# Row normalization on one core: 16 tiles of 8 rows in six buffers, in place of tiles of 12 rows in four

## The chip, the cores and the metric

The kernel runs on one core of a Trainium2 chip. The core has several engines with instruction queues of their own. Three matter here: DVE (VectorE), which does the arithmetic; ACT (ScalarE), which does a little of it and issues the stores; and SP (SyncE), which issues the loads. The transfers themselves run on 16 DMA engines that both queues share. The metric is the time of one execution on the device, in microseconds (us); lower is better.

## The reference

```python
def setup_inputs():
    batch, seq, dim = 32, 512, 1024
    return {"x": np.random.randn(batch, seq, dim).astype(np.float32)}

def reference(x):
    sums = np.sum(np.abs(x), axis=-1, keepdims=True)
    return (x / (sums + 1e-8)).astype(np.float32)
```

Each of the 16384 rows of 1024 floats (4 KB) is divided by the sum of its absolute values. Input and output are 67.11 MB each, and every byte is read once and written once.

## The kernel before

The 16384 rows are spread over the 128 partitions of the on-chip memory, so each partition has 128 rows to do, in 11 tiles: ten of 12 rows per partition (48 KB) and a last one of 8 rows (32 KB). Four tile buffers (`BUFS = 4`) hold 4 x 48 KB = 192 KB of each partition.

The function `piece` says which rows of the input and output a tile covers. The first 128 x 32 rows are the head: in it each partition owns 32 consecutive rows, which make up tiles 0 and 1 (12 rows each) and the last tile (8 rows). Behind the head each tile of 12 rows is a block of its own, in which each partition owns 12 consecutive rows. A row of a partition in the tile thus starts 128 KB from the next partition's in the head, and 48 KB behind it.

`load(i)` (line 82) issues a tile's load on SP, `store(i)` (line 85) its store on ACT. Both limit the contiguous piece that one DMA packet moves to 24576 bytes: a tile of 12 rows goes out as two packets of 24 KB per partition, and the tile of 8 rows as two of 16 KB. One transfer is spread over the 16 DMA engines, 8 partitions on each.

`normalize` computes a tile in place: a reduction over the rows on DVE (line 47), two small instructions on the sums (lines 54 and 56, adding the epsilon and taking the reciprocal), and then the products. The table `split` gives for a tile how its rows are shared out. By default one DVE instruction multiplies all rows by their reciprocals (line 58). For tiles 0, 1, 2 and the last two, some rows are instead done one at a time, by DVE (line 65) or by ACT (line 68); an entry (3, 4) means three rows by line 65 and four by line 68.

The order is written out by hand: four loads first, then for each tile compute, store, and the load of the tile four further on. That load reuses the buffer, so SP waits until the store from that buffer has landed. DVE waits for each tile's load; ACT issues a store when the tile's products are done. The loads form one queue (q1 in the profile), the stores another (q10).

Of the kernel before, what the change touches and what calls it, by code (L numbers as in the profile page):

```python
# [1 line left out]

# [4 lines left out]

FP32 = mybir.dt.float32
EPS = 1e-8


@with_exitstack
def kernel(
    ctx: ExitStack,
    tc: tile.TileContext,
    x: bass.AP,
    out: bass.AP,
):
    nc = tc.nc
    P = nc.NUM_PARTITIONS  # L20

    x_flat = x.flatten_outer_dims()
    out_flat = out.flatten_outer_dims()
    n, d = x_flat.shape

    R = 12
    BUFS = 4
    HEAD = 32
    per_partition = n // P
    assert n % P == 0 and (per_partition - HEAD) % R == 0  # L30
    rows = [R] * ((per_partition - HEAD) // R + 2) + [HEAD - 2 * R]

    def piece(flat, i):
        head = flat[: P * HEAD, :].rearrange("(p r) d -> p r d", p=P)
        if i < 2:
            return head[:, R * i : R * (i + 1), :]
        if i == len(rows) - 1:
            return head[:, 2 * R :, :]
        a = P * (HEAD + R * (i - 2))
        return flat[a : a + P * R, :].rearrange("(p r) d -> p r d", p=P)  # L40

    sbuf = ctx.enter_context(tc.tile_pool(name="sbuf", bufs=BUFS))
    stats = ctx.enter_context(tc.tile_pool(name="stats", bufs=len(rows)))

    def normalize(x_tile, k, kv, kt):
        s = stats.tile([P, R], FP32)
        nc.vector.tensor_reduce(  # L47
            out=s[:, :k],
            in_=x_tile[:, :k, :],
            axis=mybir.AxisListType.X,  # L50
            op=mybir.AluOpType.add,
            apply_absolute_value=True,
        )
        nc.vector.tensor_scalar_add(out=s[:, :k], in0=s[:, :k], scalar1=EPS)  # L54
        inv = stats.tile([P, R], FP32)
        nc.vector.reciprocal(out=inv[:, :k], in_=s[:, :k])  # L56
        if kv:
            nc.vector.tensor_mul(  # L58
                out=x_tile[:, :kv, :],
                in0=x_tile[:, :kv, :],  # L60
                in1=inv[:, :kv].unsqueeze(2).to_broadcast([P, kv, d]),
            )
        for r in range(kv, kv + kt):
            row = x_tile[:, r, :]
            nc.vector.tensor_scalar_mul(out=row, in0=row, scalar1=inv[:, r : r + 1])  # L65
        for r in range(kv + kt, k):
            row = x_tile[:, r, :]
            nc.scalar.activation(  # L68
                out=row,
                in_=row,  # L70
                func=mybir.ActivationFunctionType.Copy,
                scale=inv[:, r : r + 1],
            )

    last = len(rows) - 1
    split = {0: (3, 4), 1: (0, 3), 2: (0, 3), last - 1: (0, 2), last: (5, 3)}

    tiles = {}

    def load(i):  # L80
        x_tile = tiles[i] = sbuf.tile([P, R, d], FP32, name="x_tile")
        nc.sync.dma_start(out=x_tile[:, : rows[i], :], in_=piece(x_flat, i), max_dma_last_dim=24576)  # L82

    def store(i):
        nc.scalar.dma_start(out=piece(out_flat, i), in_=tiles[i][:, : rows[i], :], max_dma_last_dim=24576)

    def compute(i):
        k = rows[i]
        kt, ks = split.get(i, (0, 0))
        normalize(tiles[i], k, k - kt - ks, kt)  # L90

    with tc.manual_schedule():
        for i in range(BUFS):
            load(i)
        for i in range(len(rows)):
            compute(i)
            store(i)
            if i + BUFS < len(rows):
                load(i + BUFS)


# [1 line left out]
_INS = ['x']  # L103
_OUTS = [((32, 512, 1024), 'float32')]


# [23 lines left out]
```

## Time and profile before

| | |
|---|---|
| time, median of 3 runs | 316.91 us (316.88 to 317.0) |
| time of the profiled execution | 316.94 us |
| its span | 315.3 us |
| DVE busy | 261.2 us, 83% of the span |
| ACT busy | 17.4 us, 6% |
| DMA queue of the loads, share of the 16 engines' span | 49.9% |
| DMA queue of the stores | 49.4% |
| bytes moved | 134.22 MB, 426 GB/s over the span |
| load of a tile of 12 rows, issue to landing (median) | 37.3 us |
| store of a tile of 12 rows, issue to landing (median) | 47.4 us |

The span runs from the first to the last instruction that the profile shows; the time of the execution is slightly more. Busy time on an engine is the sum of its instructions. The shares of the two DMA queues count the time of their packets against 16 engines over the whole span, so that together they tell how full the DMA engines were. In tables by window, each line gives a stretch of the span, the busy time of DVE, ACT and POOL in it (with the number of instructions), a clock that plays no part here, the DMA share and the rate at which bytes moved. In tables of instructions, `s` are the sums, `inv` the reciprocals, and the shapes are partitions x elements.

### The profile page before, as it was taken

The numbers are of one execution on the slowest core, as the hardware profiler recorded it, in microseconds if no ns is written. First come the engines' busy times: TensorE is split into PE (matmuls) and PEld (weight loads), VectorE is DVE, ScalarE is ACT, GpSimd is POOL, SyncE is SP. The second block draws the span as 40 slices with busy tenths as digits, with TensorE's granted clock in tenths as the row PEclk, the third lists the DMA queues.
The fourth block names the chain that finished last, engine by engine and source line by source line (L and its number), as shares of the span: only waits on it lengthen the run. The fifth ranks groups of instructions, "written<-read, shape, count | busy, mean of one in ns | idle before, by whom it ended". The sixth has DMA issues, their size and how long they took to land.

```text
span 315.3 us, 168 instructions
## 1 busy us (share of the span) xinstructions
DVE 261.2 (83%) x51; ACT 17.4 (6%) x16; POOL 0.2 (0%) x4
## 2 busy tenths in 40 slices
DVE  0079999999999999979996997999699969999100
ACT  0010503004000000000000000000000000203000
POOL 0000000000000000000000000000000000000000
DMA  7999999999999999999999999999999999999997
GB/s 299 449 440 408 449 393 415 440 449 418 430 449 418 430 449 418 430 449 421 427 449 421 427 449 424 424 449 433 415 449 436 412 448 419 446 417 449 440 408 333
DMA packets 5984, 134.22 MB, mean 426 GB/s; under 512 B 352, under 2 KB 352, under 8 KB 352
## 3 DMA queue, kind: packets, MB, share of 16 engines
q1 hardware_dynamic: 2992, 67.11, 49.9%
q10 hardware_dynamic: 2992, 67.11, 49.4%
HBM read 67.11 MB, written 67.11 MB: 426 GB/s over the span
## 4 chain that ended last, share of the span: by engine, by line
DVE 41%; DMA 33%; another core or an unknown queue 18%; SPq 0%; issue 0%; DVEq 0%
DVE s L47 23%; DMA x_tile<-in_x_dram 17%; DVE x_tile L58 15%; DMA out_dram<-x_tile 15%; DVE x_tile L65 1%; DVE inv L56 0%; DVE s L54 0%; SPq L82 0%; DVEq L125 0%
## 5 line engine op out<-in xcount | busy, mean ns | idle before, releaser
L47 DVE TENSOR_REDUCE s<-x_tile 128x12 f32<-128x12288 f32 (+1 forms) x11 | 138.2, 12562 | 30.1 <-DMA x_tile<-in_x_dram 30.1
L58 DVE TENSOR_TENSOR x_tile<-x_tile,inv 128x12288 f32<-128x12288 f32 (+3 forms) x10 | 113.6, 11358 | 0.5
L68 ACT ACTIVATE x_tile<-x_tile,inv 128x1024 f32<-128x1024 f32 x15 | 16.1, 1138 | 257.1 <-DVE inv L56 257.1
L65 DVE TENSOR_SCALAR x_tile<-x_tile,inv 128x1024 f32<-128x1024 f32 x8 | 5.5, 747 | 0.0
L56 DVE RECIPROCAL inv<-s 128x12 f32<-128x12 f32 (+1 forms) x11 | 2.5, 225 | 0.4
L68 ACT ACT_TABLE_LOAD x1 | 1.3, 1283 | 17.9 <-DMA x_tile<-in_x_dram 17.9
L54 DVE TENSOR_SCALAR s<-s 128x12 f32<-128x12 f32 (+1 forms) x11 | 1.9, 172 | 0.4
L114 POOL MEMSET const-bfloat16-1.0<- 128x1 bf16 x1 | 0.1, 101 | 0.0
L114 POOL MEMSET const-uint8-127<- 128x1 uint8 x1 | 0.1, 101 | 0.0
L114 POOL MEMSET const-float32-0.0<- 128x1 f32 x1 | 0.1, 98 | 0.2 <-issue 0.2
L114 POOL MEMSET const-float32-1.0<- 128x1 f32 x1 | 0.1, 98 | 0.0
## 6 DMA issues: line engine op xcount, KB each, us to landing
x_tile<-in_x_dram SPq DMA_DIRECT2D x10, 6144.0 KB, 37.3
out_dram<-x_tile ACTq DMA_DIRECT2D x10, 6144.0 KB, 47.4
x_tile<-in_x_dram SPq DMA_DIRECT2D x1, 4096.0 KB, 32.5
out_dram<-x_tile ACTq DMA_DIRECT2D x1, 4096.0 KB, 21.6
```

What stands on the lines that cost most here:

```text
L47: nc.vector.tensor_reduce(out=s[:, :k], in_=x_tile[:, :k, :], axis=mybir.AxisListType.X, op=mybir.AluOpType.add, apply_absolute_value=True,)
L54: nc.vector.tensor_scalar_add(out=s[:, :k], in0=s[:, :k], scalar1=EPS)
L56: nc.vector.reciprocal(out=inv[:, :k], in_=s[:, :k])
L58: nc.vector.tensor_mul(out=x_tile[:, :kv, :], in0=x_tile[:, :kv, :], in1=inv[:, :kv].unsqueeze(2).to_broadcast([P, kv, d]),)
L65: nc.vector.tensor_scalar_mul(out=row, in0=row, scalar1=inv[:, r : r + 1])
L68: nc.scalar.activation(out=row, in_=row, func=mybir.ActivationFunctionType.Copy, scale=inv[:, r : r + 1],)
L114: nc = _bacc.Bacc("TRN2", target_bir_lowering=False, num_devices=1)
```

## The change

All tiles now have 8 rows per partition: 16 equal tiles instead of eleven, in six buffers of 32 KB instead of four of 48 KB (again 192 KB per partition). The limit on the packet size is gone from the load and the store, so the 32 KB that a partition contributes to a tile are one contiguous piece for one descriptor. The head is gone too. Instead, every three consecutive tiles form a group in which each partition owns 24 consecutive rows (96 KB); the sixteenth tile is a group by itself, in which a partition owns 8 rows (32 KB). In `split`, the entries for tiles 0, 1 and 2 are smaller, in keeping with the smaller tiles; those of the last two tiles stay. The reduction, the small instructions and the loops are as before.

```diff
-    R = 12
-    BUFS = 4
-    HEAD = 32
+    R = 8
+    BUFS = 6
+
+    GROUP = 3
     per_partition = n // P
-    assert n % P == 0 and (per_partition - HEAD) % R == 0
-    rows = [R] * ((per_partition - HEAD) // R + 2) + [HEAD - 2 * R]
+    assert n % P == 0 and per_partition % R == 0
+    rows = [R] * (per_partition // R)
 
     def piece(flat, i):
-        head = flat[: P * HEAD, :].rearrange("(p r) d -> p r d", p=P)
-        if i < 2:
-            return head[:, R * i : R * (i + 1), :]
-        if i == len(rows) - 1:
-            return head[:, 2 * R :, :]
-        a = P * (HEAD + R * (i - 2))
-        return flat[a : a + P * R, :].rearrange("(p r) d -> p r d", p=P)
+        g = i // GROUP
+        size = min(GROUP, len(rows) - g * GROUP) * R
+        a = P * g * GROUP * R
+        j = (i - g * GROUP) * R
+        own = flat[a : a + P * size, :].rearrange("(p r) d -> p r d", p=P)
+        return own[:, j : j + R, :]
...
-    split = {0: (3, 4), 1: (0, 3), 2: (0, 3), last - 1: (0, 2), last: (5, 3)}
+    split = {0: (2, 3), 1: (0, 2), 2: (0, 2), last - 1: (0, 2), last: (5, 3)}
...
-        nc.sync.dma_start(out=x_tile[:, : rows[i], :], in_=piece(x_flat, i), max_dma_last_dim=24576)
+        nc.sync.dma_start(out=x_tile[:, : rows[i], :], in_=piece(x_flat, i))
...
-        nc.scalar.dma_start(out=piece(out_flat, i), in_=tiles[i][:, : rows[i], :], max_dma_last_dim=24576)
+        nc.scalar.dma_start(out=piece(out_flat, i), in_=tiles[i][:, : rows[i], :])
```

## The prediction, on record before the changed kernel ran

> **What bounds the kernel now.** I read the page first: who is busy, and whether the DMA engines ever stop.
>
> ```profile
> DVE 261.2 (83%) x51; ACT 17.4 (6%) x16; POOL 0.2 (0%) x4
> DMA  7999999999999999999999999999999999999997
> DMA packets 5984, 134.22 MB, mean 426 GB/s; under 512 B 352, under 2 KB 352, under 8 KB 352
> q1 hardware_dynamic: 2992, 67.11, 49.9%
> q10 hardware_dynamic: 2992, 67.11, 49.4%
> ```
>
> The two queues (q1 the loads of SP, q10 the stores of ACT) fill 99.3% of the 16 DMA engines' time, against 83% of DVE's. Of 5984 packets 352 are tiny: one per engine at the end of each of 22 transfers. The other 5632 are 352 for each engine, 320 of 24 KB (twenty transfers of 12 rows: 8 partitions, two each) and 32 of 16 KB (two of 8 rows). So the end is set by how long an engine takes for its packets, and by the time in which it has none. The windows show both; their last two columns are DMA share and GB/s.
>
> ```profile
> 0.00:4.00 4.00, 0.00 (x0) 0.00 (x0) 0.20 (x4) 1.00 0.62 197
> 40.00:44.00 4.00, 4.00 (x1) 0.00 (x0) 0.00 (x0) 1.00 0.95 319
> 60.00:240.00 180.00, 169.54 (x28) 3.23 (x3) 0.00 (x0) 1.00 1.00 433
> 305.20:312.50 7.30, 0.00 (x0) 0.00 (x0) 0.00 (x0) 1.00 1.00 431
> ```
>
> From 60 to 240 us, all 24 KB packets, the rate is flat at 433 GB/s: 16 x 24576 B / 433 = 908.1 ns per packet on an engine. At the end, all 16 KB packets, it is 431: 608.2 ns. An engine's packets therefore take 320 x 908.1 + 32 x 608.2 ns = 310.05 us. The head loses 2.2 us (197 x 4 / 433 = 1.8 us of work in 4), and the stretch at 40 us, where the first store's packets join the loads, 1.05 us. That makes 313.3; the remaining 2.0 us of the 315.3 lie behind the last packets. The program's own time in this execution is 316.94, 1.64 around the span and 0.03 over the median shown.
>
> Then the costs on DVE by shape, and the end in order of time, since only there can the queue run dry.
>
> ```profile
> L47 DVE TENSOR_REDUCE s<-x_tile 128x12 f32<-128x12288 f32 x10 | 129.5, 12949 | 30.1 <-DMA x_tile<-in_x_dram 30.1
> L58 DVE TENSOR_TENSOR x_tile<-x_tile,inv 128x9216 f32<-128x9216 f32 x2 | 19.5, 9758 | 0.1
> L58 DVE TENSOR_TENSOR x_tile<-x_tile,inv 128x5120 f32<-128x5120 f32 x1 | 5.5, 5491 | 0.0
> L65 DVE TENSOR_SCALAR x_tile<-x_tile,inv 128x1024 f32<-128x1024 f32 x8 | 5.5, 747 | 0.0
> L47 DVE TENSOR_REDUCE s<-x_tile 128x8 f32<-128x8192 f32 x1 | 8.7, 8686 | 0.0
> ```
>
> ```profile
> 280.01 8.69 DVE L47 TENSOR_REDUCE s<-x_tile 128x8 f32<-128x8192 f32 x1
> 280.11 0.38 ACTq L85 DMA_DIRECT2D out_dram<-x_tile  x1
> ...
> 289.18 3.40 DVE L65 TENSOR_SCALAR x_tile<-x_tile,inv 128x1024 f32<-128x1024 f32 x5
> 292.66 0.38 ACTq L85 DMA_DIRECT2D out_dram<-x_tile  x1
> ```
>
> DVE waits 30.1 us for loads, none the other way in mid-run. The last store goes out at 292.66, when some 20.6 us of packets are left (to 313.3), of which its own are 32/2 x 0.608 = 9.7: it came 11 us before the queue would have been empty.
>
> **The change, part by part.** *Packets.* An engine has 256 of 32 KB in place of 352. No row has one of 32 KB. From both sides: by the straight line through the two sizes 908.1 + (908.1 - 608.2) = 1208.0 ns; in proportion, with no fixed part saved, 908.1 x 4/3 = 1210.8. The 431 is rounded and its window short, so I take the middle, 1209.4: 256 x 1209.4 = 309.61 us, a gain of 0.45 (0.8 at one end, 0.1 at the other).
>
> The Trainium skill ("DMA: Bandwidth & Descriptors", section Specifications) puts the fabric's ceiling at 435 GB/s, by which all the bytes take 308.4 us; the 433 of the trace leaves little for any descriptor size to win.
>
> *Transfers.* 32 in place of 22: each engine has ten more closing packets. In the window from 60 to 240 a dozen transfers end without a dent in the 433 (its rounding is 0.2 us over the window, so at most 0.02 us each): 0 to 0.2, I take 0.05. The five more issues each on SP and ACT (0.38 us) lie on queues that mostly wait.
>
> A rule speaks against this part: the same page (Anatomy of one DMA) gives each transfer about 2.0 us of fixed cost; ten more in the open would mean some 337 us. Here both rings stay filled while a completion is under way, and the flat 433 says that it is hidden.
>
> *DVE.* A full tile costs 8.69 (reduction) + 0.17 + 0.20 (the small rows) + 8 rows of product. Two product rows give (9.758 - 5.491)/4 = 1.067 us a row and 0.16 on top: 8.69. With 0.1 for gaps 17.85 us, against DMA's 2 x 8 x 1.2094 = 19.35 for a load and a store. So DVE still waits, 1.5 us a tile; its sixteen reductions and 20 more instructions lie under the packets. If that cover went, each 0.1 us that a tile took beyond 19.35 would cost up to 1.6 us in all.
>
> *Buffers and queues.* Both kernels have 48 rows in flight. In the built program load 5 waits on load 0's semaphore, which costs nothing: SP waits at 13 us while loads 1 to 4 fill the ring. Stores 9 and 10 come to wait on ACT for the landing of loads 10 and 11, whose semaphores they share; behind them on ACT are only later stores, and the store ring holds more than a tile: nothing.
>
> *The end.* This is where it could break. A tile's store lands s us after its issue. After the last load's landing the ring has (s - 3.7)/2 us of work: store 14 was issued 3.7 earlier (1.5 of idle, two rows on ACT), and while loads run stores get half the rate. Until the last store's first packet it takes 8.69 + 0.17 + 0.20 + 0.1 + 5 x 0.68 + 1.1 (issue to packet) = 13.7. So the queue runs dry if s is below 31.1. What s is follows from the head: load 0 takes 16/2 x 1.21 = 9.7 plus the 3.3 that the first one has now over its packets (17.85 - 14.5), then tile 0 costs 9.1 on DVE, 3 rows of product (3.4) and two of 0.75, so store 0 goes out at 27.1. In the kernel before store 0 went out at 38.87 and load 4, which waits for its landing, at 73.05; 29.1 us of alternating packets before that is 43.9, so its first packet came 4.8 to 5 us late. With 4.8: stores land at 51.3 + 19.35k, loads (2.85 tiles in by then) at -3.9 + 19.35k, stores go out 17.95 behind: s = 37.3, a margin of 3.1 us. If its packets came 1.1 behind the issue, s = 29.9 and 0.6 us is lost.
>
> *Addresses.* Rows of one partition now lie 96 KB from the next one's (32 KB in the last tile); before 48 and, in the head, 128. Both of those run at the full rate (the 10 us windows from 10 to 30, with the head's 128 KB, have 433 as well), so 0; a dearer pitch would show in the last tile alone.
>
> Sum: 316.94 - 0.45 + 0.05 = 316.5.
>
> **The rivals.** *The starts shrink* (faster). The 1.05 us at 40 and about 0.4 of the head are packets drawn out while a stream begins; smaller tiles begin the stores earlier and might spare them: 316.5 - 1.05 = 315.5. For it: nothing else in the trace departs from 433. Against: the first store still meets a filled load ring.
> *The end runs dry* (slower). Place: between store 14's last packet and store 15's first; it decides from s below 31.1. Price (31.1 - s)/2: at the smallest s, a store's own transfer at half rate, 19.35, it is 5.9 (322.4); the middle is 2.9: 319.4. Against it stands the margin above.
> *A 32 KB piece doesn't travel as one packet* (slower; the change doesn't do what it says). As two of 16 KB: 512 x 608.2 = 311.4, or 1.35 more than now: 318.2. The page would count 8192 packets of data. For it: no row shows one above 24 KB.
>
> **How the numbers follow.** About 0.2% (0.6 us) is what a measurement of this kernel can tell from no change: under 316.3 is faster, over 317.5 slower. Forecast 0.59 (its own range 316.0 to 317.0: 0.47 same, 0.12 faster); starts shrink 0.17, faster; dry end 0.13 and split packets 0.11, slower. Together faster 0.29, same 0.47, slower 0.24. The likeliest gives 316.5. From 315.4 to 318.2 the range takes in the shrunk starts and the split packets and leaves out most of the dry end and a little below.
>
> **What would show it.** 4096 packets of data; 433 GB/s in mid-run, not less; DVE waiting about 1.5 us before each reduction; the last store issued with 2 to 4 us of the previous one left, no window below 400 GB/s between 285 and 312. I am wrong if the mid-run rate changes (packet or address cost), if windows near 300 fall (dry end), or if dips like the one at 40 us come several times or not at all.

## The result and the profile after

The changed kernel takes 317.86 us (median of 8 runs, 317.74 to 317.91) against 316.99 for the kernel before (8 runs, 316.88 to 317.26): a ratio of 1.0025, with a 95% interval of 1.0016 to 1.0035. Ratios and intervals, here and below, leave out runs more than 1.5% above the fastest of their kernel; only e15 has any, three of its six. Forecast was 316.5, with a range up to 318.2. The kernel became 0.87 us slower where 0.4 of gain was forecast, and the direction is clear of the interval.

The first view is the page of the changed kernel: busy times, DMA packets, queues.

```profile
DVE 268.0 (85%) x70; ACT 14.3 (5%) x13; POOL 0.2 (0%) x4
DMA packets 4609, 134.23 MB, mean 425 GB/s; under 512 B 512, under 2 KB 512, under 8 KB 512
q1 hardware_dynamic: 2304, 67.11, 49.8%
q10 hardware_dynamic: 2304, 67.11, 49.2%
q14 instruction: 1, 0.01, 0.0%
```

There are 4096 packets of data and 512 closing ones (the tiny packet with which an engine ends its share of a transfer): a 32 KB piece does travel as one packet. New is the last row. One packet of 8 KB on a queue that the kernel doesn't use, named `instruction`: the core fetched the next part of an instruction stream while the kernel ran. The page before had no such row.

The windows of the changed kernel, columns as before (DMA share and GB/s at the end):

```profile
0.00:4.00 4.00, 0.00 (x0) 0.00 (x0) 0.20 (x4) 1.00 0.73 254
20.00:40.00 20.00, 19.79 (x10) 5.42 (x5) 0.00 (x0) 1.00 0.99 398
60.00:240.00 180.00, 168.04 (x40) 0.00 (x0) 0.00 (x0) 1.00 1.00 434
290.00:300.00 10.00, 9.90 (x8) 3.21 (x3) 0.00 (x0) 1.00 0.97 419
300.00:310.00 10.00, 0.19 (x1) 0.02 (x1) 0.00 (x0) 1.00 1.03 446
```

Mid-run is as good as before (434 against 433), and the end doesn't run dry: 419 and 446 average to the full rate. The short windows swing, since a packet on each of the 16 engines is 0.5 MB and counts whole in the window in which it starts. The stretch in which the first store joins the loads is now the one from 20 to 40 us, at 398. In the kernel before it is this one:

```profile
30.00:50.00 20.00, 19.90 (x8) 4.26 (x4) 0.00 (x0) 1.00 1.00 414
```

Against 433 that is a loss of 0.9 us before (19/433 x 20) and 1.6 after, though the swing of whole packets is in both. The packet records of the trace tell more. Chained by engine, and with the steady distance from start to start (908 ns for 24 KB, 1209 for 32 KB, 607 for 16 KB) taken off, they show these parts, in us (some 0.2 to 0.3 us of small pieces and later starts of single engines are not listed):

| | before | after |
|---|---|---|
| first packet starts | 1.79 | 1.73 |
| packets at the steady distance, closing ones included, per engine | 310.1 | 309.7 |
| drawn out in the head, mean of 16 engines | 0.67 | 0.61 |
| drawn out at the first store, mean | 0.91 | 1.35 |
| engines end, mean | 313.70 | 313.69 |
| slowest engine ends | 313.89 | 314.52 |
| second slowest | 313.88 | 313.92 |
| last landing to the end of the program | 2.72 | 2.96 |
| profiled execution (span) | 316.94 (315.3) | 317.89 (315.7) |

So the packets gained their 0.4 us, and the first store took it back: the engines end at the same time in the mean. Then one engine is 0.6 behind the rest, and the program takes 0.24 more to end. That is nearly the whole difference. The engine that is late is the one that carried the fetch. The view of the DMA queues in a window of 1 us, 243 to 244 us, has it:

```profile
q1 hardware_dynamic: 16, 0.52, 124.7%
q14 instruction: 1, 0.01, 1.9%
q10 hardware_dynamic: 3, 0.00, 0.2%
```

In the packet records it starts at 243.48 us and takes 309 ns; the data packet behind it on the same engine takes 1751 ns where its like take 1213. Together that sets this engine back by 0.85 us; without it, it would have ended at 313.67, close to the mean of the others. In the kernel before a packet of 8 KB on this queue comes at 315.95, behind the span and all the data.

### The profile page after: what moved, and what is told of

It reads as the page before. It is cut to its first block, busy times and chain, and to the rows that moved or that the text cites. A ratio compares the mean times of both kernels' runs of the same rounds, so it can differ in the third digit from the quotient of the medians.

```text
span 315.7 us, 203 instructions
## 1 busy us (share of the span) xinstructions
DVE 268.0 (85%) x70; ACT 14.3 (5%) x13; POOL 0.2 (0%) x4
## 4 chain that ended last, share of the span: by engine, by line
DVE 85%; another core or an unknown queue 5%; DMA 4%; issue 0%; DVEq 0%
DVE s L47 44%; DVE x_tile L58 38%; DMA x_tile<-in_x_dram 4%; DVE x_tile L65 1%; DVE inv L56 1%; DVE s L54 1%; DVEq L125 0%; DVEq L58 0%
## 5 line engine op out<-in xcount | busy, mean ns | idle before, releaser
L47 DVE TENSOR_REDUCE s<-x_tile 128x8 f32<-128x8192 f32 x16 | 139.0, 8684 | 30.4 <-DMA x_tile<-in_x_dram 30.4
L58 DVE TENSOR_TENSOR x_tile<-x_tile,inv 128x8192 f32<-128x8192 f32 (+2 forms) x15 | 118.6, 7910 | 0.7
L68 ACT ACTIVATE x_tile<-x_tile,inv 128x1024 f32<-128x1024 f32 x12 | 13.0, 1140 | 272.7 <-DVE inv L56 272.7
L65 DVE TENSOR_SCALAR x_tile<-x_tile,inv 128x1024 f32<-128x1024 f32 x7 | 4.8, 750 | 0.0
L56 DVE RECIPROCAL inv<-s 128x8 f32<-128x8 f32 x16 | 3.2, 203 | 0.5
L54 DVE TENSOR_SCALAR s<-s 128x8 f32<-128x8 f32 x16 | 2.8, 172 | 0.6
```

The source lines that it names most:

```text
L47: nc.vector.tensor_reduce(out=s[:, :k], in_=x_tile[:, :k, :], axis=mybir.AxisListType.X, op=mybir.AluOpType.add, apply_absolute_value=True,)
L58: nc.vector.tensor_mul(out=x_tile[:, :kv, :], in0=x_tile[:, :kv, :], in1=inv[:, :kv].unsqueeze(2).to_broadcast([P, kv, d]),)
L68: nc.scalar.activation(out=row, in_=row, func=mybir.ActivationFunctionType.Copy, scale=inv[:, r : r + 1],)
```

## The experiments

Four theories were put to the test. *Fetch*: the 8 KB packet delays one engine, which then ends last. *ACT's instructions*: what lies between the last landing and the end of the program grows with ACT's instruction stream. *First store, by size*: the loss there grows with the packet. *First store, by moment*: it depends on when the store joins. Times are medians of all runs of a kernel; the kernel before had 317.12, 317.0, 317.03 and 317.05 in the four groups that follow (e1 to e4, e5 to e8, e9 to e11, e12 to e15), and 316.85 in one run beside e16 and e17.

**e1, fewer DVE instructions.** Edit to the changed kernel:

```diff
-        nc.vector.tensor_scalar_add(out=s[:, :k], in0=s[:, :k], scalar1=EPS)
```

> The changed kernel with the addition of the epsilon (line 54) left out: sixteen instructions of DVE fewer, nothing else. Theory 'fetch': the changed kernel's instruction stream is long enough that 8 KB of it are fetched in mid-run (the page's row q14, one packet), and that packet draws out one data packet on one DMA engine (1751 ns for 1213 at 243.8 us), which then ends 0.6 us behind the others and sets the end. With fewer instructions on DVE the fetch comes later or not before the end: no row q14, last packet near 313.9 instead of 314.5, span some 0.6 us shorter (315.1), time 317.2 to 317.4. Rival 'DVE is not it' (the fetch belongs to another engine, or is harmless): row q14 stays and the time stays at 317.8 to 317.9.

Measured 317.69, ratio 1.0022 (1.0013 to 1.0032). Row q14 stayed, but the fetch moved from 243 to 301 us, and the slowest engine ended at 314.38. That was not the engine with the fetch, which ended third, at 314.07. A miss in the numbers: sixteen instructions were too few. The place of the fetch does follow DVE's count: in the ten profiles with a fetch in the run it came when DVE had started 60 to 67 instructions (records with its waits; 63 in the changed kernel, 67 here), while the counts of ACT and SP at that moment ranged from 22 to 52.

**e2, the changed kernel with 16 KB packets** (`max_dma_last_dim=16384` in load and store).

> The changed kernel with its packets cut to 16 KB (two per partition and tile). Theory 'first store': the loss at the moment when the first store joins the loads is one to two packets drawn out on every engine, so it grows with the packet: 1.0 us with 24 KB, 1.4 with 32 KB, so 0.6 to 0.7 here. The packets themselves cost 512 x 607 to 608 ns per engine, 1.2 to 1.5 us more than 256 of 1209. Sum: +0.5 to +0.8 over the changed kernel, 318.4 to 318.7. Rival 'the loss is fixed or due to the six loads in flight': it stays at 1.4, and the time goes to 319.1 to 319.4.

Measured 318.74, ratio 1.0052 (1.0037 to 1.0067), just above what the size theory said; the first store lost 1.04, between both theories.

**e3, the kernel before with 48 KB packets** (24576 becomes 49152).

> The kernel before with its packets enlarged to 48 KB (one per partition and tile; 32 KB in the last tile). Theory 'first store': packets save 160 x 5 ns = 0.8 us per engine, and the loss at the first store doubles from 1.0 to about 2 us, the one at the head may grow too: +0.2 to +0.6, 317.1 to 317.6. Rival 'the loss does not depend on the packet': 0.8 us shorter than before, 316.1 to 316.3.

Measured 316.94, ratio 0.9999 (0.9983 to 1.0015), single runs from 316.4 to 319.0: between both theories. In the profiled run (317.61) the first store lost 1.33 in place of 0.91. The mean of the engines ended at 313.38, 0.3 earlier than before, and four engines 0.6 to 1.2 behind it. In this profile larger packets gain in the mean of the engines and lose in their evenness.

**e4, the kernel before with as many DVE instructions as after.**

```diff
+        for _ in range(PADS):
+            nc.vector.memset(pad, 0.0)
```

(`PADS` is 2, behind each tile's `normalize`; `pad` is a scratch tile of 8 columns.)

> The kernel before with two clearings of a scratch tile of 8 columns after each of the 11 tiles: 22 instructions of DVE more, as many as the changed kernel has; some 0.1 us each, in time in which DVE waits for loads anyway. Theory 'fetch': a row q14 appears in the span, one data packet is drawn out by some 0.5 us, and the time grows by 0.5 to 1.1 us to 317.4 to 318.1 (the larger figure if the time outside the span grows with the instructions too: it was 1.63 before and 2.15 after). Rival 'DVE is not it': no row q14, time 316.9 to 317.1.

Measured 317.68, ratio 1.0019 (1.0009 to 1.0028). The page of this kernel, before's but for the padding, now has the packet:

```profile
DMA packets 5985, 134.23 MB, mean 425 GB/s; under 512 B 352, under 2 KB 352, under 8 KB 352
q1 hardware_dynamic: 2992, 67.11, 49.8%
q10 hardware_dynamic: 2992, 67.11, 49.3%
q14 instruction: 1, 0.01, 0.0%
```

It starts at 245.17 us. Its engine is the slowest and ends at 314.52, the next at 313.83: 0.7 in place of the 0.6 after the change, with the old tiles. The last landing to the end takes 2.71 (2.72 before), so DVE's count isn't behind that term. Fetch is shown from this side.

**e5, the changed kernel with a short DVE stream.**

```diff
-        nc.vector.tensor_scalar_add(out=s[:, :k], in0=s[:, :k], scalar1=EPS)
-        inv = stats.tile([P, R], FP32)
-        nc.vector.reciprocal(out=inv[:, :k], in_=s[:, :k])
+        inv = s
```

> The changed kernel without its two small instructions per tile (lines 54 and 56); the products multiply by the sums instead of their reciprocals. DVE then has fewer instructions than in the kernel before (36 against 48, merged rows not counted). Theory 'fetch': no row q14 within the span, no engine that ends 0.6 us behind the others, and the time falls by 0.4 to 0.7 from the changed kernel's 317.86 to 317.2 to 317.5 (the last tile's DVE work is 0.4 us shorter too, but the queue has 2 to 3 us of cover there, so this is worth nothing). Rival 'the fetch does not set the end' (only the loss at the first store does): 317.7 to 317.9.

Measured 317.29, ratio 1.0009 (0.9999 to 1.0018). Its page ends the DMA part like this:

```profile
DMA packets 4608, 134.22 MB, mean 426 GB/s; under 512 B 512, under 2 KB 512, under 8 KB 512
q1 hardware_dynamic: 2304, 67.11, 49.8%
q10 hardware_dynamic: 2304, 67.11, 49.4%
```

4608 packets, no row q14, the slowest engine 0.14 behind the next (313.79 and 313.65), and 0.57 us less than the changed kernel. Fetch is shown from the other side too; 0.27 of its gain can be the first store, which lost 1.08 in this profiled run.

**e6, more ACT instructions in the kernel before** (`pad` as in e4, cleared once by POOL).

```diff
+            if 3 <= i <= 8:
+                nc.scalar.activation(out=pad, in_=pad, func=mybir.ActivationFunctionType.Copy)
```

> The kernel before with six more instructions of ACT on a scratch tile of 8 columns, one behind each of the stores of tiles 3 to 8 (ACT idles there). Open is why 2.96 us lie between the last landing and the end of the program after the change and 2.72 before. Theory 'ACT's instructions': the time around the span grows from 1.64 to about 1.9 to 2.15, time 317.1 to 317.4. Rival 'transfers' or anything else: the time around the span stays at 1.6 to 1.7 and the time at 316.9 to 317.1.

Measured 317.52, ratio 1.0017 (1.0007 to 1.0027): above the range given. The data phase of the profiled run is that of the kernel before (slowest engine 313.89); the time around the span went from 1.64 to 2.03 (1.98 to 2.08 in the ten runs).

**e7, more transfers in the kernel before.**

```diff
+            if i == len(rows) - 3:
+                for j in range(10):
+                    nc.sync.dma_start(out=pad[:1, 8 * j : 8 * j + 8], in_=x_flat[:1, 8 * j : 8 * j + 8])
```

> The kernel before with ten more loads of 32 bytes on SP, issued behind the last real load: 32 transfers as after the change, with hardly any bytes. Theory 'transfers' (what lies around the span grows with the number of transfers or of SP's instructions): the time around the span rises to 1.9 to 2.15, time 317.2 to 317.5. Rival 'ACT's instructions': it stays at 1.6 to 1.7, time 316.9 to 317.1. Ten closing packets on one engine cost below 0.2 us in both.

Measured 318.92, ratio 1.0063 (1.0048 to 1.0078), which neither expected; but the time around the span stayed at 1.62, so the number of transfers is not behind that term. The 1.9 us are a side effect that the timeline shows:

```profile
224.03 52.15 ACTq L85 DMA_DIRECT2D out_dram<-x_tile  x2
...
247.79 28.75 SPq L104 DMA_DIRECT2D pad<-in_x_dram  x10
...
276.30 2.19 ACT L68 ACTIVATE x_tile<-x_tile,inv 128x1024 f32<-128x1024 f32 x2 [197.75 <-DMA pad<-in_x_dram]
280.10 0.38 ACTq L85 DMA_DIRECT2D out_dram<-x_tile  x1
```

The first line merges stores 7 and 8: the second went out at 275.8, though its products were done at 253.1. A semaphore is a counter that a transfer raises when it lands; eight of them go round among the loads and stores of this program. The small loads had taken some of them, and their packets lay behind the last real load in the queue. Store 8 shared its semaphore (number 106) with one of them and waited for it, as the ACT product behind it did (the bracket in the third line). So the store ring (the stores' packets that are issued and not yet moved; the loads have a ring of their own) ran empty, the last load's packets ended at 275.1, and the first of store 8 came at 276.7. The window from 270 to 280 fell from 433 GB/s to 354. This is a dry stretch like the one feared at the end, made by accident.

**e8, the kernel before with 16 KB packets** (24576 becomes 16384).

> The kernel before with its packets cut to 16 KB (three per partition and tile of 12 rows). Packets: 512 x 607 to 608 ns, 0.9 to 1.3 us more per engine than before. Theory 'first store grows with the packet': the loss there falls from 0.9 (24 KB) to 0.5 to 0.7, time 317.5 to 318.1. Rival 'it does not depend on the packet but on the buffers' (the changed kernel with 16 KB packets lost 1.0): it stays at 0.9 and the time is 317.9 to 318.4; if it were as with six buffers, above that.

Measured 317.73, ratio 1.0023 (1.0013 to 1.0034), first store some 0.6: as the size theory has it. With four buffers and store 0 near 38.9 us, the loss is 0.6, 0.78 to 1.0 (five profiles, e15's among them) and 1.33 for 16, 24 and 48 KB.

**e9, the kernel before without ACT's products** (`split = {}`).

> The kernel before with an empty split: DVE does all the products with one instruction per tile, ACT only issues the stores (15 products and a table load fewer on ACT, two instructions fewer on DVE). Theory 'ACT's instructions' (six more cost 0.4 us around the span): the time around the span falls below 1.6, by 0.3 to 0.6, and the time to 316.3 to 316.8. The last tile's products take 8.7 us in place of 3.4 on DVE, the one before it 2.1 more; the last store goes out near 300, while the store before it has packets until 304: no loss there. Rival 'only instructions beyond some number cost': around the span 1.6 as before, time 316.9 to 317.1. If the store queue did run dry, the windows near 304 would fall below 430.

Measured 318.48 (317.11 to 319.05), ratio 1.0041 (1.0026 to 1.0056): a miss. In the profiled run (317.11) 2.74 us lie behind the last landing, as before: 23 fewer ACT records gain nothing. Store 0 went out at 44.3, so that the load ring was empty when load 4 was issued, and packets were drawn out again near 80 us. Why most runs took a microsecond more than the profiled one isn't known.

**e10, the changed kernel with ACT's products in the last tile only** (`split = {last: (5, 3)}`).

> The changed kernel with the entries of split for tiles 0, 1, 2 and the last but one left out: nine products of ACT fewer, and DVE does them. Theory 'ACT's instructions': the time around the span falls from 2.15 to 1.5 to 1.7, the fetch in mid-run stays (DVE has hardly fewer instructions), time 317.3 to 317.5. Rival 'the time around the span comes from the tiles or transfers': it stays at 2.15 and the time at 317.8.

Measured 317.04, ratio 1.0015 (0.9996 to 1.0034), nine runs of twelve between 316.84 and 317.35, three up to 320.26. The time around the span fell to 1.74 to 1.83 in all of them (1.5 to 1.7 expected): ACT's instructions, in the changed kernel itself. The time fell by more than expected, because the window of the first store improved as well:

```profile
20.00:40.00 20.00, 19.79 (x8) 0.00 (x0) 0.00 (x0) 1.00 1.00 418
```

418 in place of 398, with the same 32 KB packets and a store 0 at 30.9 instead of 26.9 us. In the records the loss is 0.75 against 1.35. Size alone is refuted. The fetch is still there (240.39 us), but its engine ended second, at 313.85; another, without a fetch, ended at 314.10.

**e11, both streams short** (e1's edit and `split = {last: (0, 3)}`).

> The changed kernel with both streams shortened: the addition of the epsilon left out (line 54), split only for the last tile, and there five rows by one DVE instruction and three by ACT. DVE has about as many instructions as before the change, ACT fewer. If the fetch (0.6) and ACT's instructions (0.3 to 0.4) are the two terms that I missed beside the first store, this gives 316.7 to 317.0, no different from the kernel before within 0.1%: the packets' gain of 0.4 against the loss of 0.4 at the first store. If another term was missed, it stays above 317.2.

Measured 318.07 (317.21 to 320.7), ratio 1.0065 (1.0039 to 1.0091): a miss. The profiled run (317.21) has no fetch in the span, 2.59 behind the last landing and 0.78 at the first store, and an engine mean of 313.19, half a microsecond better than before. But one engine ended at 314.28, the next at 313.35; one of the late engine's packets had taken 1620 ns at 132 us, without any fetch. So a fetch isn't the only thing that sets one engine back.

**e12, e13, e14: moment or size.** Edits to `split` in the changed kernel:

```diff
-    split = {0: (2, 3), 1: (0, 2), 2: (0, 2), last - 1: (0, 2), last: (5, 3)}
+    split = {0: (0, 0), 1: (0, 2), 2: (0, 2), last - 1: (0, 2), last: (5, 3)}   # e12
+    split = {0: (2, 3), last - 1: (0, 2), last: (5, 3)}                         # e13
+    split = {0: (5, 3), 1: (0, 2), 2: (0, 2), last - 1: (0, 2), last: (5, 3)}   # e14
```

> The changed kernel with tile 0's products all in one DVE instruction: store 0 goes out near 30.8 instead of 26.9, with the same 32 KB packets. Theory 'moment' (the run with fewer ACT products lost only 0.75 at the first store, with 32 KB packets and a store 0 at 30.9): the loss at the first store falls from 1.35 to 0.7 to 0.9; ACT has four instructions fewer, the fetch stays; time 317.1 to 317.5. Theory 'size' (the loss is one to two packets drawn out, whatever the moment): it stays at 1.1 to 1.4, time 317.6 to 317.9.

> The changed kernel without ACT's products in tiles 1 and 2; store 0 goes out at 26.9 as in the changed kernel. Theory 'moment': the loss at the first store stays at 1.1 to 1.4; the time around the span falls to 1.7 to 1.9 (fewer instructions on ACT); time 317.4 to 317.7. Theory 'ACT's products in the head cause the loss': it falls to 0.7 to 0.9 here too, time 317.0 to 317.3.

> The changed kernel with five rows of tile 0 done singly by DVE (3.5 us in place of 4.8): store 0 goes out near 25.7. Theory 'moment': the loss at the first store changes with the place in the load ring at which the first store arrives; 1.2 us earlier than in the changed kernel is one packet, so it lies between 0.7 and 1.7, time 317.5 to 318.2. Theory 'size': 1.1 to 1.4, time 317.8 to 317.9.

| | store 0 issued | lost at the first store | time, ratio (interval) |
|---|---|---|---|
| e12 | 31.0 | 1.08 | 317.74 (316.89 to 319.33), 1.0020 (1.0006 to 1.0034) |
| e13 | 26.8 | 1.42 | 317.40 (317.21 to 317.77), 1.0011 (1.0002 to 1.0019) |
| e14 | 25.6 | 1.14 | 317.51 (317.32 to 317.96), 1.0018 (1.0009 to 1.0027) |

The window from 20 to 40 us of e13 and of e12, in this order:

```profile
20.00:40.00 20.00, 19.79 (x10) 3.23 (x3) 0.00 (x0) 1.00 0.99 401
```

```profile
20.00:40.00 20.00, 19.82 (x7) 1.28 (x1) 0.00 (x0) 1.00 1.01 413
```

e13 keeps the moment and the loss; ACT's products in tiles 1 and 2 are not its cause. e12 moves the moment and loses less, though not as little as e10: 1.08 lies between the theories, and the time of 317.74 is the one of the size theory (e16 and e17 below tell more of it). e14 moves it the other way and loses 1.14, which both theories allowed. e13 also has the time around the span at 1.75 to 1.83 where the changed kernel has 2.15: of the 0.46 by which it is faster than the changed kernel, 0.36 lie there.

**e15, large packets but small ones at the start.** In the kernel before:

```diff
+    def limit(i, first):
+        return 24576 if i < first or i == last else 49152
...
-        nc.sync.dma_start(out=x_tile[:, : rows[i], :], in_=piece(x_flat, i), max_dma_last_dim=24576)
+        nc.sync.dma_start(out=x_tile[:, : rows[i], :], in_=piece(x_flat, i), max_dma_last_dim=limit(i, 5))
...
-        nc.scalar.dma_start(out=piece(out_flat, i), in_=tiles[i][:, : rows[i], :], max_dma_last_dim=24576)
+        nc.scalar.dma_start(out=piece(out_flat, i), in_=tiles[i][:, : rows[i], :], max_dma_last_dim=limit(i, 3))
```

> The kernel before with packets of 48 KB, except in loads 0 to 4, stores 0 to 2 and the last tile, which keep 24 and 16 KB. Theory: the loss at the first store stays at 0.8 to 0.9 as with 24 KB, the packets save 112 x 5 ns = 0.56 us, time 316.3 to 316.6 against 317.0. Rival 'larger packets leave the engines further apart at the end' (the run with 48 KB throughout had one engine 1.1 us behind the mean): 316.6 to 317.4.

Measured: ratio 1.0075 (1.0046 to 1.0105), single runs from 318.58 to 324.12. A clear miss. The profiled run took 323.57; its timeline and a window:

```profile
282.00 0.34 ACTq L88 DMA_DIRECT2D out_dram<-x_tile  x1
296.98 8.69 DVE L47 TENSOR_REDUCE s<-x_tile 128x8 f32<-128x8192 f32 x1 [15.05 <-DMA x_tile<-in_x_dram]
...
309.63 0.39 ACTq L88 DMA_DIRECT2D out_dram<-x_tile  x1
```

```profile
300.00:310.00 10.00, 9.45 (x8) 3.23 (x3) 0.00 (x0) 1.00 0.40 172
```

The last load, issued at 250.3 in 16 KB packets, ran beside stores of 48 KB and landed 46.6 us later (32.5 before, beside 24 KB); DVE waited 15 us, and the queue stood empty for some 6 us (172 against 433 over 10 us). The packet records show two causes. On every engine the two queues took turns packet by packet, 16 KB against 48: by that, 15 of the 16 engines were through with the load at 291.2 to 291.6 us, some 41 us after its issue. The sixteenth was a packet behind, its 48 KB packets took up to 2.4 us in place of 1.8 from 275 us on, and it was through at 296.6. So of the 14 us more, some 9 are the unequal packets and 5 are one slow engine, for which the trace shows no cause. It is the prediction's dry end, in the kernel before. The two shortest runs are 5 us shorter, which is what the lack of the slow engine would give; they have no profile, so this is not shown.

The turns agree with what the Trainium skill states ("DMA: Bandwidth & Descriptors", section Queues, rings and completion order): an engine takes turns between its queues by the packet. There a packet is a group of descriptors; here each turn is one piece of 16 or 48 KB. So the queue with the larger packets gets the larger share.

**e16, e17, e12's kernel once more, twice.**

> The kernel of e12 once more, for one look: half of its runs took 318 to 319, its profiled one 317.06. If this look falls on a long one: theory 'end' (the last load lands late, the store queue runs dry): a window between 295 and 306 below 380 GB/s. Theory 'engines' (one or a few DMA engines lose packets' time in mid-run): windows near 300 full, and the last landing 1 to 2 us behind the mean of the engines. If it is near 317, it says nothing.

> A second look at the kernel of e12, with the same two theories: where the time is 318 or more, an end that runs dry shows a window between 295 and 306 below 380 GB/s, and engines that lose time in mid-run show full windows near 300 and a last landing 1 to 2 us behind the engines' mean.

Measured 317.66 and 317.46. The windows from 295 to 306 of e16 and e17 have 438 and 444 GB/s, so the end didn't run dry. The engines end at 313.3 in the mean in both, the slowest at 314.73 and 314.52: the scatter seen here is single engines. In neither is the slowest the one with the fetch, which ended at 313.85 and 313.86. The runs of 318 to 319 have no profile; their cause stays open. The first store lost some 0.9 in both.

## Why the prediction was wrong

**What held.** The packets: the steady distance is 1209 ns, where 1209.4 was taken, and the 0.4 us per engine were gained. The mid-run at the full rate, in spite of ten more transfers, whose closing packets take an engine 6 ns each (0.05 us was taken for all ten). The section that the prediction quotes for 2.0 us a transfer is about transfers that GpSimd issues; here SP and ACT issue them. DVE's wait of 1.5 us before each reduction from 113 us on, and the end, shown by the changed kernel's timeline:

```profile
248.87 8.69 DVE L47 TENSOR_REDUCE s<-x_tile 128x8 f32<-128x8192 f32 x1 [1.52 <-DMA x_tile<-in_x_dram]
...
284.05 0.34 ACTq L85 DMA_DIRECT2D out_dram<-x_tile  x1
287.62 8.69 DVE L47 TENSOR_REDUCE s<-x_tile 128x8 f32<-128x8192 f32 x1 [3.67 <-DMA x_tile<-in_x_dram]
...
300.28 0.34 ACTq L85 DMA_DIRECT2D out_dram<-x_tile  x1
```

Store 14 went out 3.6 us ahead of the last landing (3.7 forecast), the last store at 300.28. With 1.1 us to its first packet it was ready at 301.4, while store 14's packets lasted until 304.0 in the mean of the engines (it landed at 305.27): a margin of some 2.6 us (3.1 forecast). The s of 37.3 us was met by store 12: out at 247.39, landed at 284.72.

**What was luck.** The 317.86 lies within the range, but the range's upper end came from packets split in two, and the chance given to "slower" from that and the dry end. Neither happened.

**What failed is the sum.** It ended with 316.94 - 0.45 + 0.05, that is, it carried everything else of the old execution over unchanged. Three terms were not unchanged.

First, "its sixteen reductions and 20 more instructions lie under the packets". Their execution does, as the waits show. But instructions have to be fetched too, through the same 16 DMA engines, and the longer stream brought a fetch into the run: 0.85 us on one engine, which then ended 0.6 behind the others and set the end (e4 puts it into the old kernel, e5 takes it out of the new). The trace of before had no row of this kind within its span, so it couldn't be read there.

Second, "1.64 around the span" was taken as a constant. It is one of the kernel, not of the chip: from the last landing to the end of the program it takes 2.93 to 2.96 us in e1, e2, e5, e14 and the changed kernel, which all have 55 ACT records in the trace (with waits), and 3.10 in e6, the kernel before padded to 55; with 50 or fewer (e3, e4, e7 to e13 and e15 to e17, and the kernel before with 49) it is 2.59 to 2.74. The net is 0.24. From like to like it is more: six records more cost 0.38 (e6 against the kernel before), seven fewer save 0.37 (e13 against the changed kernel). Why, the profile doesn't show, and fewer than 48 gained nothing more (26 in e9: 2.74).

Third, the 1.05 us at the first store, kept as they were. The rival "the starts shrink" had its mechanism in the right place and the sign wrong: smaller tiles do begin the stores earlier, and at 26.7 to 26.9 us the loss is 1.31 to 1.42 (three profiles), against 0.78 to 1.0 with the old kernel's 24 KB at 38.9. With 32 KB and a store 0 at 30.7 to 31.0 it is 0.75 to 1.08 (five profiles), and at 26.5 and 25.6 us 1.08 and 1.14 (e5, e14). So part is the moment. Part is size: 16 to 48 KB at nearly one moment make 0.6 to 1.33 (e8, e3). One profile varies from another of its like by up to 0.3, and no run here changes the number of loads in flight (six in place of four) by itself, so the 0.44 are not split further.

Together: 0.6 + 0.24 + 0.44 lost, 0.4 gained by the packets and 0.1 in the head and at the first packet, makes some +0.8 of the 0.95 between the profiled executions. The prediction's own split of the old execution put the end of the packets at 313.3 with 2.0 us behind it; the records have the slowest engine at 313.9, and 1.4 us. The sum didn't rest on that.

The rival "a 32 KB piece doesn't travel as one packet" is out by the packet count, and "the end runs dry" by the margin; e15 shows that such an end exists, with some 6 us of empty queue (5.9 was its highest price), 5 of them by one slow engine.

No version tried here is clearly faster than the kernel before; e3 comes level with it in the median and e10 in most runs.

## What to carry to other kernels

When a queue is full from end to end, the time is its packets plus whatever disturbs single engines, the start and the end; a change worth half a microsecond has to be weighed against those small terms, and what lies around the span is one of them. Count instructions per engine even where their execution is hidden: their fetch uses the DMA engines that the data uses. Where two queues share the engines, give them packets of like size (e15), and look at the last load first: it decides when the last store can start.

## What the runs showed of the hardware that was not expected

- A fetch of 8 KB of instructions within the run (row q14) sets the DMA engine that serves it back by up to 0.85 us (309 ns of its own, and 1751 ns for a packet of 1213). The 16 engines don't make up for one another: in the changed kernel and e4 this engine ended 0.6 and 0.7 us behind the next, and the kernel without the fetch was some 0.6 us faster (e5 against the changed one, the kernel before against e4). Where another engine was late for other reasons (e1, e10, e16, e17), the fetch didn't set the end. It came when DVE had started 60 to 67 instructions: at 243.5, 245.2 and 301.3 us in kernels with 86, 86 and 70 DVE records, behind the end in the seven kernels with 64 (the kernel before among them), and not at all with 57 and 54 (e9, e5). The Trainium skill speaks of cache lines of 16 KB or 256 instructions, two of them ("Advanced Engine Details and Errata", section ISA Cache); here 8 KB at a time were fetched.
- The fixed part of a data packet is only some 5 ns: steady distances of 607, 908 and 1209 ns for 16, 24 and 32 KB are 301 ns per 8 KB and 5 over.
- Packets that alternate by number and not by bytes: beside stores in 48 KB packets a load in 16 KB ones was through after some 41 us on 15 of 16 engines, where the load beside 24 KB packets landed after 32.5 (e15).
- Eight semaphores go round among all transfers of this program. A transfer of 32 bytes held up a store by 22.7 us, because the store took the same semaphore and the transfer lay behind a load of 4 MB (e7).
